# A two-block transformer kernel in split float32: high weights pass once over the operand's high and low halves side by side, and a second, normalised operand

## The chip, the cores and the metric

The kernel runs on one core of one Trainium2 chip, as one launch. The metric is the device time of a launch in microseconds (us), here a median of three. A core has a matrix engine (TensorE, PE in the rows), three engines for elementwise work (VectorE or DVE, ScalarE or ACT, GpSimd or POOL), SyncE (SP), which here only issues the transfers of the weights, a memory SBUF of 128 partitions, and the accumulators of TensorE, PSUM, of which this kernel uses eight banks of 128 x 512 float32.

## The reference

256 tokens, width 1024, feed-forward width 2816, two blocks of two layers each. Every layer is a mixer and a feed-forward, each behind an RMS norm and added to the residual `h`:

```python
def _rmsnorm(x, g):
    return x * lax.rsqrt(jnp.mean(x * x, axis=-1, keepdims=True) + EPS) * g
def _token_mixer(xn, ...):                                   # block 1, both layers
    u, q, k, v, g_pool, g_attn = jnp.split(xn @ w_in, SPLITS, axis=-1)
    pooled = centred means of u over windows (2, 4, 8, 16), a quarter of the width each, minus u
    pool_out = (pooled @ w_pool, group by group) * pool_scale
    attn_out = three dilated local attentions over q, k, v (4 heads of 128 each), mixed by their lse
    return (sigmoid(g_pool) * (pool_out @ w_a) + sigmoid(g_attn) * (attn_out @ w_b)) @ w_o
def _conv_ffn(xn, w_up, conv_w, conv_b, w_down):             # block 2: silu, and a causal convolution
    a, gval = jnp.split(xn @ w_up, 2, axis=-1)
    a = depthwise convolution of a over 3 tokens + conv_b
    return (gelu(a) * gval) @ w_down
```

Block 2 has an even layer (HGRN2 recurrence and an S5 state space side by side) and an odd layer (latent attention) in place of the token mixer.

## The kernel before

Activations lie feature-major: `h` is [128 features, 8 tiles, 256 tokens]. TensorE multiplies in float32r, which keeps fewer bits than float32, so each operand of the large products is a high part and a low part: `X[0]` is the rounded value and `X[1]` what is left, and so with weights. A weight piece of up to 128 x 1024 float32 is fetched by SP's queue (`raw`), ScalarE casts it to the high part `whi` (L170), and VectorE subtracts for the low part `wlo` (L172); each of the three has four buffers. A product is three passes (`mm3`, L187 to L189):

```python
nc.tensor.matmul(out, lhsT=a[0], rhs=b[0], start=start, stop=False)   # high weight, high operand
nc.tensor.matmul(out, lhsT=a[0], rhs=b[1], start=False, stop=False)   # high weight, low operand
nc.tensor.matmul(out, lhsT=a[1], rhs=b[0], start=False, stop=stop)    # low weight, high operand
```

With the weight as the stationary side (128 x 128) and the 256 tokens as moving columns, a weight tile is three matmuls of 256 columns into one half of a bank. `chunkA` does this for two feature tiles of a stage's output (16 weight tiles, 48 matmuls, two pieces of weights). Four banks are there for it. Value projections (`chunkB`) take the tokens as the stationary side and 512 weight columns as moving ones; for the first attention group (`nat`) the tokens stand side by side, for the other two (`par`) they are every second one.

`Norm.feed` makes the operand `X` of the next stage as soon as a tile of `h` is made: h times the norm's gain, split. The factor 1/rms of a token isn't in it. It is known when the last tile is done; `Norm.finish` spreads it over the partitions as `rb` (L296), and whoever takes a result out of PSUM multiplies by `rb` (VectorE), or scales by its column `rs` (the values, ScalarE). So a stage starts without waiting for the norm; its first three chunks (`chunksA`) leave the last two operand tiles to the end. The feed-forward loop over 22 chunks is, for each:

```python
nc.vector.tensor_tensor(ag, ps, bc2(rb), op=ALU.mult)          # L526: both halves, convolution and gate
nc.scalar.activation(c, a, AF.Identity, scale=w[j0], ...)      # L531: middle tap and bias
nc.vector.scalar_tensor_tensor(out=c[:, o], in0=a[:, s_], ...) # L539: twice, the other two taps
nc.scalar.activation(c, c, act)                                # L541
nc.gpsimd.tensor_tensor(c, c, ag[:, 1, :], op=ALU.mult)        # L542: times the gate
nc.scalar.copy(ah[:, i, :], c)                                 # L543: high part
nc.gpsimd.tensor_tensor(al[:, i, :], c, ah[:, i, :], ...)      # L544: low part
```

The down-projection follows: 8 output tiles, 22 weight tiles each, one VectorE addition to `h` (L569), and the feed of the next stage. In the feed-forward of block 1's second layer GpSimd also works through the parameters of S5 (`side`, from L659 on), one or two steps behind each low part. `EdgeNorm` is the norm between the blocks. The tile framework's scheduler sets the order of the instructions on each engine and the semaphores; every engine works through its own list in order.

## Time and profile before

| | |
|---|---|
| timed, median of 3 | 1569.27 us (1568.94 to 1570.26) |
| profiled execution, span from first to last instruction | 1566.8 us |
| what lies between them | 2.5 us |
| TensorE: a matmul under way | 1519.9 us, 97%, 12596 matmuls |
| VectorE busy | 1066.2 us, 68% |
| ScalarE busy | 779.6 us, 50% |
| GpSimd busy | 613.3 us, 39% |
| read from device memory | 256.45 MB, 164 GB/s over the span |

No total is recorded for the profiled execution beside its span, so the median minus the span stands for what lies around it. Busy time is the sum of recorded durations, with overlaps counted once; it is an average over stages that differ, and an engine that is busy half of the span may be the one waited for in a stage of 80 us.

### The profile page before, as it was taken

The page shows a single profiled execution, that of the slowest core. Times are in us where ns is not written, and L with a number is a line of the kernel's source. Part 1 is how long each engine was busy: PE and PEld are TensorE (multiplying, and loading weights), DVE is VectorE, ACT ScalarE, POOL GpSimd, SP SyncE. Part 2 cuts the span into 40 slices and gives each one's busy share as a digit, 9 for nine tenths or more (in the row PEclk, how much of TensorE's full clock was granted, in tenths as well). Part 3 has the DMA queues.
Part 4 walks back from the last instruction along what each step waited for, and adds up shares of the span by engine and source line. Part 5 has one row for each costly group of instructions (what it writes and reads, how often), then busy time and mean ns, then how long its engine had stood idle before and what let it go on. Part 6 is the DMA issues. An engine that isn't in the chain of part 4 may idle for free.

```text
span 1566.8 us, 30996 instructions
## 1 busy us (share of the span) xinstructions
PE 1519.9 (97%) x12596; PEld 1482.1 (95%) x12596; DVE 1066.2 (68%) x1384; ACT 779.6 (50%) x1192; POOL 613.3 (39%) x606
## 2 busy tenths in 40 slices
PE   9999999999999999999988799999999998999997
PEld 8899999999999999999977799999999997999997
DVE  6756566766666566648587587978766667776754
ACT  4644444555444544445544444456555445565542
POOL 5500023333336000224999984444433312333332
PEclk9999999999999999999999999999999999999999
DMA  8554355555464643565443265335554554355553
GB/s 254 188 181 148 127 176 187 186 187 174 159 208 156 219 163 134 169 195 185 150 136 134 88 196 191 109 115 177 188 188 151 184 181 138 106 182 185 172 161 112
DMA packets 90542, 260.07 MB, mean 166 GB/s; under 512 B 17688, under 2 KB 28840, under 8 KB 90400
## 3 DMA queue, kind: packets, MB, share of 16 engines
q1 hardware_dynamic: 78688, 254.05, 49.4%
q10 hardware_dynamic: 11552, 3.73, 1.1%
q8 instruction: 98, 1.61, 0.4%
q14 instruction: 44, 0.36, 0.1%
q0 software_dynamic: 160, 0.32, 0.1%
HBM read 256.45 MB, written 1.10 MB: 164 GB/s over the span
## 4 chain that ended last, share of the span: by engine, by line
PE 77%; POOL 11%; DVE 7%; issue 2%; DMA 1%; ACT 1%; DVEq 0%; ACTq 0%; POOLq 0%
PE ps_mm L187 24%; PE ps_mm L189 24%; PE ps_mm L188 24%; DVE wlo L172 3%; POOL tm L708 1%; POOL al L544 1%; POOL cv L542 1%; DVE xl L247 1%; PE ps_sm L443 1%; POOL s5c L709 1%; POOL s5b L709 1%; ACT whi L170 1%; DVE h L474 1%; POOL s5b L707 1%; POOL s5c L707 1%
## 5 line engine op out<-in xcount | busy, mean ns | idle before, releaser
L172 DVE TENSOR_TENSOR wlo<-raw,whi 128x1024 fp32r<-128x1024 f32 (+3 forms) x536 | 649.8, 1227 | 275.9 <-ACT whi L170 268.4
L170 ACT CAST whi<-raw 128x1024 fp32r<-128x1024 f32 (+3 forms) x536 | 509.7, 958 | 427.0 <-PE ps_mm L188 342.6
L189 PE MATMUL ps_mm<-xh,wlo 128*128 128x256 f32 x2352 | 671.7, 286 | 14.7 <-DVE wlo L172 14.5
L187 PE MATMUL ps_mm<-xh,whi 128*128 128x256 f32 x2352 | 669.6, 285 | 3.4 <-DVE gate L464 1.7
L188 PE MATMUL ps_mm<-xl,whi 128*128 128x256 f32 x2352 | 670.2, 285 | 0.8 <-DVE xl L247 0.8
L189 PEld LDWEIGHTS ps_mm<-xh,wlo 128*128 128x128 f32 x2352 | 453.4, 193 | 18.2 <-DVE wlo L172 18.2
L187 PEld LDWEIGHTS ps_mm<-xh,whi 128*128 128x128 f32 x2352 | 453.6, 193 | 4.8 <-ACT whi L170 3.5
L188 PEld LDWEIGHTS ps_mm<-xl,whi 128*128 128x128 f32 x2352 | 453.7, 193 | 3.2 <-DVE xl L247 2.9
L189 PE MATMUL ps_mm<-ah,wlo 128*128 128x256 f32 x704 | 199.3, 283 | 1.6 <-DVE wlo L172 1.6
L187 PE MATMUL ps_mm<-ah,whi 128*128 128x256 f32 x704 | 199.3, 283 | 0.6 <-ACT whi L170 0.6
L188 PE MATMUL ps_mm<-al,whi 128*128 128x256 f32 x704 | 199.2, 283 | 0.0
L542 POOL TENSOR_TENSOR cv<-cv,ag 128x256 f32<-128x256 f32 x88 | 115.4, 1312 | 211.8 <-ACT cv L541 191.3
L465 POOL TENSOR_TENSOR gate<-gate 128x256 f32<-128x256 f32 x16 | 20.0, 1258 | 343.3 <-DVE gate L464 343.3
L259 POOL TENSOR_TENSOR sq<-h 128x256 f32<-128x256 f32 (+1 forms) x47 | 70.5, 1499 | 184.7 <-DVE h L569 93.4
L189 PEld LDWEIGHTS ps_mm<-ah,wlo 128*128 128x128 f32 x704 | 135.2, 192 | 1.8 <-DVE wlo L172 1.8
L187 PEld LDWEIGHTS ps_mm<-ah,whi 128*128 128x128 f32 x704 | 135.2, 192 | 0.8 <-ACT whi L170 0.8
L188 PEld LDWEIGHTS ps_mm<-al,whi 128*128 128x128 f32 x704 | 135.2, 192 | 0.0
L539 DVE SCALAR_TENSOR_TENSOR cv<-ag,vec,cv 128x255 f32<-128x255 f32 (+1 forms) x176 | 102.0, 579 | 20.1 <-ACT cv L531 17.1
L543 ACT CAST ah<-cv 128x256 fp32r<-128x256 f32 x88 | 35.8, 407 | 136.3 <-POOL cv L542 136.2
L544 POOL TENSOR_TENSOR al<-cv,ah 128x256 fp32r<-128x256 f32 x88 | 75.4, 857 | 34.6 <-ACT ah L543 34.1
L526 DVE TENSOR_TENSOR ag<-ps_mm,rb 128x512 f32<-128x512 f32 x88 | 60.5, 687 | 40.2 <-PE ps_mm L189 39.8
L531 ACT ACTIVATE cv<-ag,vec 128x256 f32<-128x256 f32 x88 | 52.6, 598 | 26.2 <-POOL al L544 18.9
(342 smaller groups left out, 2127.1 us busy)
## 6 DMA issues: line engine op xcount, KB each, us to landing
raw<-w_up SPq DMA_DIRECT2D x88, 512.0 KB, 3.6
raw<-w_fi SPq DMA_DIRECT2D x88, 512.0 KB, 3.7
raw<-w_qk SPq DMA_DIRECT2D x48, 512.0 KB, 3.6
raw<-w_gate SPq DMA_DIRECT2D x32, 512.0 KB, 3.6
raw<-w_down SPq DMA_DIRECT2D x32, 512.0 KB, 3.5
raw<-w_fo SPq DMA_DIRECT2D x32, 512.0 KB, 3.6
raw<-w_v SPq DMA_DIRECT2D x24, 512.0 KB, 4.5
raw<-w_u SPq DMA_DIRECT2D x16, 512.0 KB, 6.0
```

Source lines behind the costliest of these rows:

```text
L170: nc.scalar.copy(self.hi[:, :n], raw[:, :n])
L172: eng.tensor_tensor(self.lo[:, :n], raw[:, :n], self.hi[:, :n].bitcast(F32), op=ALU.subtract)
L187: nc.tensor.matmul(out, lhsT=a[0], rhs=b[0], start=start, stop=False)
L188: nc.tensor.matmul(out, lhsT=a[0], rhs=b[1], start=False, stop=False)
L189: nc.tensor.matmul(out, lhsT=a[1], rhs=b[0], start=False, stop=stop)
L259: nc.gpsimd.tensor_tensor(q, hs, hs, op=ALU.mult)
L526: nc.vector.tensor_tensor(ag, ps, bc2(rb), op=ALU.mult)
L531: nc.scalar.activation(c, a, AF.Identity, scale=w[j0], bias=cb[:, i:i + 1])
L539: nc.vector.scalar_tensor_tensor(out=c[:, o], in0=a[:, s_], scalar=w[j], in1=c[:, o], op0=ALU.mult, op1=ALU.add)
L542: nc.gpsimd.tensor_tensor(c, c, ag[:, 1, :], op=ALU.mult)
L543: nc.scalar.copy(ah[:, i, :], c)
L544: last = nc.gpsimd.tensor_tensor(al[:, i, :], c, ah[:, i, :].bitcast(F32), op=ALU.subtract)
```

## The change

An operand is one tile now, [128, k, 2, 256], with the high and the low part of a feature tile next to each other (`Pair`). Where the weight is the stationary side, `mmW` makes one matmul of 512 columns with the high weight over both parts, and one of 256 with the low weight over the high part: a weight tile is two matmuls. The first lands in both halves of a bank, and the low weight's is put on the right half; `fold` adds the halves at evacuation: ScalarE copies the right half out, VectorE adds it to the left one. A chunk (`chunkW`) fills two banks in place of one. The bank's halves can't be multiplied by `rb` and added in one instruction, so these stages read a second operand, `xn`, that has 1/rms in it already (`normalised`): eight steps on VectorE, ScalarE and GpSimd each, in every stage that has such chunks (two mixers, the even layer, four feed-forwards). The first three chunks of a stage and the pool projections, the merges and the output projections keep the three passes (`mmX`); the values keep their form but read `xn`, and are copied out without a factor. In the down-projection seven of eight output tiles use `mmW`, with two additions to `h` on VectorE (L617 of the change); the eighth keeps the old form. The tags of the large tiles change (`b24` twice becomes `b24` and `c24`).

```diff
+        class Pair:
+            def __init__(self, t):
+                self.t = t
+                self.hl = (t[:, :, 0, :], t[:, :, 1, :])
...
+        def mmW(ps, w, X, k, nk, start=None, stop=None):
+            nc.tensor.matmul(ps, lhsT=w[0], rhs=X.t[:, k].rearrange("p a b -> p (a b)"),
+                             start=k == 0 if start is None else start, stop=False, skip_group_check=True)
+            nc.tensor.matmul(ps[:, S:], lhsT=w[1], rhs=X[0][:, k, :], start=False,
+                             stop=k == nk - 1 if stop is None else stop, skip_group_check=True)
+        def fold(out, ps, view=lambda t: t):
+            t = ap_.tile([128, S], F32, tag="ft", name="ft", bufs=3)
+            nc.scalar.copy(t, ps[:, S:])
+            nc.vector.tensor_tensor(out, view(ps[:, :S]), view(t), op=ALU.add)
...
+        def chunkW(src, X, nk=8):
+            w = Chunk(src, nk * 256)
+            pss = []
+            for m in range(2):
+                pss.append(bank())
+                for k in range(nk):
+                    mmW(pss[m], w.at((m * nk + k) * 128), X, k, nk)
+            return pss
...
+            def normalised(self):
+                Y = split_pair("xn")
+                for k in range(8):
+                    t = ap_.tile([128, S], F32, tag="ft", name="xt", bufs=3)
+                    nc.vector.scalar_tensor_tensor(out=t, in0=h[:, k, :], scalar=self.g[:, k:k + 1], in1=self.rb,
+                                                   op0=ALU.mult, op1=ALU.mult)
+                    nc.scalar.copy(Y[0][:, k, :], t)
+                    nc.gpsimd.tensor_tensor(Y[1][:, k, :], t, Y[0][:, k, :].bitcast(F32), op=ALU.subtract)
+                return Y
...
         def mixer(l, nm):
...
-            rb, rs = nm.rb, nm.rs
+            rb = nm.rb
+            Y = nm.normalised()
...
-            v_group(l, 0, X, rs, qkv)
+            v_group(l, 0, Y, qkv)
...
-                qk_head(l, j, X, rb, qkv)
+                qk_head(l, j, Y, qkv)
...
-            ps = chunkA(A["w_gate"][l, m], X)
             g = ap_.tile([128, 2, S], F32, tag="gate", name="gate", bufs=3)
-            nc.vector.tensor_tensor(g, ps, bc2(rb), op=ALU.mult)
+            for i, ps in enumerate(chunkW(A["w_gate"][l, m], X)):
+                fold(g[:, i], ps)
...
         def ffn(nm, win, cw, cb, wdown, act, shifts, feed, side=None):
...
-            ah = ap_.tile([128, NF, S], F32R, tag="b24", name="ah")
-            al = ap_.tile([128, NF, S], F32R, tag="b24", name="al")
+            Y = nm.normalised()
+            hk = NF // 2
+            act_ = [Pair(ap_.tile([128, hk, 2, S], F32R, tag=t + "24", name="act", bufs=1)) for t in "bc"]
...
-                nc.vector.tensor_tensor(ag, ps, bc2(rb), op=ALU.mult)
+                if i < 3:
+                    nc.vector.tensor_tensor(ag, pss[i], bc2(rb), op=ALU.mult)
+                else:
+                    for j, ps in enumerate(chunkW(win(i), Y)):
+                        fold(ag[:, j], ps)
...
-                    mm3(pd[m][:, :S], w.at(k * 128), (ah[:, kk, :], al[:, kk, :]), kk == 0, kk == NF - 1)
+                    mmd = mmW if m < 7 else lambda ps, *a: mmX(ps[:, :S], *a)
+                    mmd(pd[m], w.at(k * 128), act_[c], k, hk, kk == 0, kk == NF - 1)
...
-                nc.vector.tensor_tensor(h[:, m, :], ps[:, :S], h[:, m, :], op=ALU.add)
+                for o in range(0, 2 * S if m < 7 else S, S):
+                    nc.vector.tensor_tensor(h[:, m, :], ps[:, o:o + S], h[:, m, :], op=ALU.add)
...
             def head_in(hd):
-                ps = chunkA(A["w_eqf"][hd], X) if hd else p0[2]
...
+                if hd:
+                    pss = chunkW(A["w_eqf"][hd], Y)
+                    fold(q[:, hd, :], pss[0])
+                    fold(f, pss[1])
...
-                ps = chunkA(A["w_eg"][c], X)
+                for m, ps in enumerate(chunkW(A["w_eg"][c], Y)):
```

Three places show what the scheduler makes of it. A row is the line, the operation, what it writes and reads, the tile's size, and how many in a row.

VectorE at the start of the first feed-forward layer, behind the sum of squares (`ms`), before:

```order
L285 TENSOR_SCALAR ms<-ps_sm 128x2
L172 TENSOR_TENSOR wlo<-raw,whi 128x1024 x3
L526 TENSOR_TENSOR ag<-ps_mm,rb 128x512
L172 TENSOR_TENSOR wlo<-raw,whi 128x1024
L539 SCALAR_TENSOR_TENSOR cv<-ag,vec,cv 128x255 x2
```

and of the change:

```order
L335 TENSOR_SCALAR ms<-ps_sm 128x2
L172 TENSOR_TENSOR wlo<-raw,whi 128x1024 x3
L313 SCALAR_TENSOR_TENSOR xt<-h,vec,rb 128x256 x3
L569 TENSOR_TENSOR ag<-ps_mm,rb 128x512
L172 TENSOR_TENSOR wlo<-raw,whi 128x1024
L313 SCALAR_TENSOR_TENSOR xt<-h,vec,rb 128x256
L569 TENSOR_TENSOR ag<-ps_mm,rb 128x512
L313 SCALAR_TENSOR_TENSOR xt<-h,vec,rb 128x256
L585 SCALAR_TENSOR_TENSOR cv<-ag,vec,cv 128x255
L313 SCALAR_TENSOR_TENSOR xt<-h,vec,rb 128x256
L172 TENSOR_TENSOR wlo<-raw,whi 128x1024
```

The eight multiplies of the normalised operand (L313) stand between the low parts of the weights and the evacuations of the first three chunks (L569), the last ones behind the first multiply-adds (L585).

ScalarE in the same layer's loop, a chunk and the start of the next, before:

```order
L170 CAST whi<-raw 128x1024
L531 ACTIVATE cv<-ag,vec 128x256
L170 CAST whi<-raw 128x1024
L541 ACTIVATE cv<-cv 128x256
L543 CAST ah<-cv 128x256
L170 CAST whi<-raw 128x1024
```

and of the change:

```order
L577 ACTIVATE cv<-ag,vec 128x256
L170 CAST whi<-raw 128x1024
L219 COPY ft<-ps_mm 128x256
L587 ACTIVATE cv<-cv 128x256
L590 CAST act<-cv 128x256
L170 CAST whi<-raw 128x1024
L219 COPY ft<-ps_mm 128x256
L577 ACTIVATE cv<-ag,vec 128x256
```

Two copies out of PSUM (L219) are in the loop, one of them between the weight cast (L170) and the middle tap (L577). The middle tap needs the addition of VectorE on that copy, which in VectorE's list stands behind the low part of that weight cast; so the loop goes from the cast L590 over L170, VectorE's low part and additions, its two multiply-adds, the activation L587, and GpSimd's multiply to the next L590.

GpSimd at the start of the feed-forward layer of block 1's second layer, before:

```order
L287 TENSOR_TENSOR rs<-ms,nhalf 128x2
L542 TENSOR_TENSOR cv<-cv,ag 128x256
L544 TENSOR_TENSOR al<-cv,ah 128x256
L659 MEMSET s5p 128x16
L660 TENSOR_SCALAR s5p<-s5p 128x16
```

and of the change:

```order
L337 TENSOR_TENSOR rs<-ms,nhalf 128x2
L316 TENSOR_TENSOR xn<-xt,xn 128x256 x7
L588 TENSOR_TENSOR cv<-cv,ag 128x256
L316 TENSOR_TENSOR xn<-xt,xn 128x256
L591 TENSOR_TENSOR act<-cv,act 128x256
L711 MEMSET s5p 128x16
```

Eight subtractions (L316) stand ahead of the first parameter step (the MEMSET of `s5p`), seven of them ahead of the loop's first multiply.

## Rows read from the trace of the kernel before

**Rows 1.** The page: span, and busy us (share) xinstructions of each engine.

```profile
span 1566.8 us, 30996 instructions
PE 1519.9 (97%) x12596; PEld 1482.1 (95%) x12596; DVE 1066.2 (68%) x1384; ACT 779.6 (50%) x1192; POOL 613.3 (39%) x606
```

**Rows 2.** Windows: us, length, busy PE PEld DVE ACT POOL, clock, DMA, GB/s.

```profile
303.80:401.40 97.60, 97.60 (x816) 97.60 (x815) 67.92 (x85) 54.34 (x85) 37.14 (x34) 1.00 0.53 174
```

**Rows 3.** Windows: block 1's second feed-forward layer, and the even layer.

```profile
800.00:884.00 84.00, 67.12 (x610) 63.63 (x609) 57.62 (x51) 37.21 (x61) 84.00 (x78) 0.92 0.36 120
1000.00:1040.00 40.00, 39.12 (x527) 36.56 (x525) 37.19 (x81) 18.45 (x43) 21.17 (x22) 1.00 0.27 93
```

**Rows 4.** Timeline of TensorE, value groups: start us, recorded us, operation, tile.

```profile
490.54 0.39 PE L187 MATMUL ps_mm<-whi,xh 128*128 128x512 f32 x1
...
501.22 0.39 PE L189 MATMUL ps_mm<-whi,xl 128*128 128x512 f32 x1
...
502.87 0.40 PE L187 MATMUL ps_mm<-whi,xh 128*128 128x512 f32 x1
...
513.82 0.40 PE L189 MATMUL ps_mm<-whi,xl 128*128 128x512 f32 x1
```

**Rows 5.** Lines by form, VectorE: count | busy us, mean ns | idle before, releaser.

```profile
L410 DVE TENSOR_TENSOR qkv<-ps_mm,rb 128x256 f32<-128x256 f32 x8 | 3.4, 424 | 3.1 <-PE ps_mm L189 2.8
L606 DVE SCALAR_TENSOR_TENSOR h<-h,vec,rb 128x256 f32<-128x256 f32 x8 | 3.3, 511 | 0.0
```

**Rows 6.** Lines by form, ScalarE and GpSimd.

```profile
L296 ACT COPY rb<-ps_sm 128x256 f32<-128x256 f32 x16 | 5.9, 370 | 3.5 <-PE ps_sm L294 3.5
L544 POOL TENSOR_TENSOR al<-cv,ah 128x256 fp32r<-128x256 f32 x88 | 75.4, 857 | 34.6 <-ACT ah L543 34.1 <-DMA raw<-w_fi 0.5
```

**Rows 7.** Timelines of three engines, a loop of the first feed-forward; [idle before <-releaser].

```profile
309.58 0.41 ACT L543 CAST ah<-cv 128x256 fp32r<-128x256 f32 x1 [1.57 <-POOL cv L542]
309.90 1.04 ACT L170 CAST whi<-raw 128x1024 fp32r<-128x1024 f32 x1
...
310.97 1.22 DVE L172 TENSOR_TENSOR wlo<-raw,whi 128x1024 fp32r<-128x1024 f32 x1 [0.63 <-ACT whi L170]
312.11 0.99 DVE L539 SCALAR_TENSOR_TENSOR cv<-ag,vec,cv 128x255 f32<-128x255 f32 x2
...
313.36 0.41 ACT L541 ACTIVATE cv<-cv 128x256 f32<-128x256 f32 x1
...
313.49 1.23 DVE L172 TENSOR_TENSOR wlo<-raw,whi 128x1024 fp32r<-128x1024 f32 x1 [0.38 <-ACT whi L170]
...
313.85 1.46 POOL L542 TENSOR_TENSOR cv<-cv,ag 128x256 f32<-128x256 f32 x1 [3.04 <-ACT cv L541]
...
315.35 0.41 ACT L543 CAST ah<-cv 128x256 fp32r<-128x256 f32 x1 [1.57 <-POOL cv L542]
```

**Rows 8.** Timelines of VectorE and ScalarE, start of the first feed-forward.

```profile
283.09 3.50 DVE L172 TENSOR_TENSOR wlo<-raw,whi 128x1024 fp32r<-128x1024 f32 x3 [1.67 <-ACT whi L170]
...
284.94 0.37 ACT L296 COPY rb<-ps_sm 128x256 f32<-128x256 f32 x1
...
303.89 0.69 DVE L526 TENSOR_TENSOR ag<-ps_mm,rb 128x512 f32<-128x512 f32 x1 [0.70 <-PE ps_mm L189]
```

**Rows 9.** Timelines of VectorE and GpSimd, block 1's second feed-forward.

```profile
729.01 3.50 DVE L172 TENSOR_TENSOR wlo<-raw,whi 128x1024 fp32r<-128x1024 f32 x3 [1.67 <-ACT whi L170]
...
738.31 0.74 POOL L542 TENSOR_TENSOR cv<-cv,ag 128x256 f32<-128x256 f32 x1 [10.17 <-PE ps_mm L189]
...
740.25 0.11 POOL L659 MEMSET s5p<- 128x16 f32 x1
...
896.35 0.72 POOL L544 TENSOR_TENSOR al<-cv,ah 128x256 fp32r<-128x256 f32 x1
```

**Rows 10.** Timelines of GpSimd and TensorE, the pool groups of the first mixer.

```profile
63.81 1.42 POOL L362 TENSOR_TENSOR pll<-pw,plh 128x512 fp32r<-128x512 f32 x1 [0.52 <-ACT plh L361]
...
66.15 0.28 PE L187 MATMUL ps_mm<-plh,whi 128*128 128x256 f32 x1
```

144 lines of the change are left out of this document (71 added, 73 removed).

## The prediction

> **What bounds the kernel now.** I read the page first. Over the span of 1566.8 us TensorE has a matmul under way for 1519.9 us, 97% [rows 1]. A matmul's recorded duration overlaps the next one's (0.28 us for one of 256 columns [rows 10]), so this says only that there is nearly always one in flight; the rate is read from counts and start times. The window row of the first feed-forward layer's loop has 816 matmuls in 97.6 us, 0.1196 us each, at a granted clock of 1.00 (the 2.4 GHz level), with no idle time [rows 2]. VectorE is busy 67.9 of these 97.6 us, ScalarE 54.3, GpSimd 37.1. So in these stretches what TensorE issues is the time, and what the other engines do is free until it gets in its way. The same view of the other stretches finds two where that is not so. From 800 to 884 us, in the feed-forward layer of block 1's second layer, GpSimd is busy 84.00 of 84.00 us and TensorE has idle time; from 1000 to 1040 us, in the even layer, VectorE is busy 37.19 of 40 us [rows 3].
>
> **What it removes.** A weight tile costs three passes now: 3 x 0.120 = 0.360 us. After the change it costs one pass of 512 columns and one of 256. The trace has 512-column matmuls in the value groups of the mixer: 48 from 490.54 to 501.22, in 47 steps of 0.227 us, where stationary columns lie side by side, and 48 from 502.87 to 513.82, in steps of 0.233, where they are taken two apart [rows 4]. Twice the columns cost 0.227 and not 0.240: about 0.013 us goes with a pass, whatever its width, and one pass per tile disappears. In the new calls the stationary columns are side by side, so I take 0.227 + 0.120 = 0.347 and save 0.013 a tile. If 0.233 held, it would be 0.007; that is the other bound.
>
> Tiles, counted from the code: up-projections 4 layers x 19 chunks x 16 = 1216; down-projections 4 x 7 x 22 = 616; q/k 2 x 4 x 3 x 16 = 384; gates 2 x 8 x 16 = 256; even layer (3 + 2) x 16 = 80. Together 2552, and 2552 x 0.013 = **33.2 us less** (17.9 by the other bound). A feed-forward layer has 458 of them (6.0 us), a mixer 320 (4.2 us).
>
> The Trainium skill, page "TensorE: Matmul & The Clock Gate", section "Back-to-back issue gap", gives N/2.4 + 2.5 ns for a warm pass, 109 and 216 ns here; a tile would go from 328 to 325 ns and the change would save 6.4 us instead of 33.2. The rows, at 120 and 227 ns, contradict it, so the sum goes by the rows.
>
> **What it adds, and what hides it.** (a) Evacuation. For a chunk VectorE had one 512-element multiply; it has two adds of 256 now, nearest row 424 ns each, and ScalarE two copies out of PSUM at 370 ns [rows 5, 6]. Per chunk of 5.55 us (16 x 0.347) VectorE goes from 4.0 (67.9 / 97.6 x 5.77) to 4.2 us and ScalarE from 3.2 to 3.9 us: both still fit, so as load they cost nothing. The second add in a down-projection (28 x 0.42 us) is hidden in the same way; it is on the end chain only for the last tile, which keeps the old form.
>
> But ScalarE's and VectorE's queues are in order, and in the new order (shown above) one loop runs through both and GpSimd. Followed from a cast of one chunk to the next chunk's cast, by rows of the old loop [rows 7]: cast to weight cast 0.32, to the low part 1.07, low part to the next instruction 1.14, add 0.42, two multiply-adds 0.99, activation 0.41, hand-over 0.08, GpSimd's multiply 1.46, hand-over 0.04: 5.93 us. GpSimd's multiply took 1.46 while VectorE made a low part beside it (313.49) and 0.74 without one (738.31) [rows 7, 9]. In the new order about 0.7 us of it meets a low part, so I take 1.3 and 5.77 us; the bounds are 5.2 and 5.93. The chunk takes TensorE 5.55 us, so the loop falls behind by 0.22 us a chunk, 4.0 us over 18. TensorE doesn't feel that at once: there are four banks, so a filled one is wanted again three halves, 8.3 us, later; copy, low part ahead, and add need some 3.1 us of it, and the start (b) eats another 1. That leaves 4. I charge 0.5 us for each of three layers, **+1.5** (0 to 8.5).
>
> (b) The normalised operand, 7 times eight steps: a VectorE multiply (nearest row 511 ns, same shape), a ScalarE cast (0.41) and a GpSimd subtraction (857 ns) [rows 5 to 7]. In a feed-forward layer the row factors arrive at 285.31 (284.94 + 0.37) and the first three chunks, on the old operand, last until 298.1 (the fourth ends at 303.89, less 5.77) [rows 8]. VectorE goes on at 286.6 (283.09 + 3.50) with the eight multiplies, three evacuations, two low parts and three multiply-adds between them: 8 x 0.51 + 3 x 0.69 + 2 x 1.22 + 3 x 0.50 = 10.1 us, to 296.7. Cast (0.41), one GpSimd multiply ahead (up to 1.46) and the last subtraction (0.86) end near 299.5, and TensorE needs that eighth part at 298.1 + 7 x 0.347 = 300.5. So there is no stall, with 1 us to spare; without that cover it would be up to 4 us a layer.
>
> (c) Block 1's second feed-forward layer. GpSimd is the bound from its first multiply, at 738.31, to its last subtraction, at 896.35 [rows 9]; it also works through the S5 parameters there. What TensorE saves in that loop, 304 x 0.013 = 4.0 us, cannot show. And GpSimd starts later: seven of the eight subtractions now stand before its first multiply, which follows VectorE's third multiply-add. From the third low part's end (729.01 + 3.50 = 732.5) VectorE does 7 x 0.51 + 2 x 0.69 + 2 x 1.22 + 3 x 0.50 = 8.9 us, to 741.4; activation 0.41, GpSimd's multiply 0.74, eighth subtraction 0.86, cast 0.41 and first subtraction 0.74 follow, so the parameter work begins near 745, not at 740.25. **+9.0** (0 if the side work is less tight than it looks, 12 if the longer VectorE queue slows GpSimd too).
>
> (d) Even layer. VectorE has 4.1 us more work on an engine that is 93% busy [rows 3], and the value matmuls now wait for the new operand. I charge all of it, **+4.1** (0 to 8).
>
> (e) Mixers. In the first mixer GpSimd makes the four pool groups one after the other, with short pauses such as the 0.52 us in the row, and the last one's low part ends at 65.23 (63.81 + 1.42); TensorE takes it up 12 matmuls after 66.15, at 67.6 [rows 10]. Eight subtractions (8 x 0.86 = 6.9 us) in front, less four such pauses that they fill, bring it to about 70: +2.5. In the other mixer the slack is larger; 0.5. **+3.0** (0 to 6). Value, q/k and gate chunks come later than the operand.
>
> **The sum.** 1566.8 - 33.2 + 1.5 + 9.0 + 4.1 + 3.0 = 1551.2 us of span. The timed median, 1569.27, lies 2.5 us above this execution's span, so **1553.7, said as 1554**. The added costs are 17.6 us, half of what is saved.
>
> **Rivals.** *A: only columns count.* If a 512-column pass cost twice a 256-column one (0.240), a tile would still cost 0.360; nothing is saved, the added work stays: 1569.3 + 17.6 = 1587. Against it: the 0.227 of [rows 4]. The skill's formula named above is nearly this case; its 6.4 us would give 1580. Chance 0.05.
>
> *B: the ScalarE-VectorE-GpSimd loop becomes the bound of the feed-forward layers.* It decides from 5.77 us a chunk; TensorE's gain is gone in all when three layers lose 15.6 us more, 5.2 each, at 5.55 + (4 + 0.5 + 5.2) / 18 = 6.1 us. At 6.4 it would be 3 x (18 x 0.85 - 4) = 34 instead of 1.5: 1586. For it: without the add the same rows sum to 5.51, so the old loop, at 5.77 [rows 7], had 0.26 us to spare, and the add takes more. Against: all its steps are rows, and they sum to 5.93 at most. The Trainium skill, page "SBUF — State Buffer", section "SBUF: two separate sides", says that VectorE and GpSimd lock a shared port pair for a whole instruction, the other blocking fully; the 1.46 beside the 0.74 agrees, and with a full block the loop would be 5.9. Chance of a time above 1566 by it: 0.13.
>
> *C: the added work hides.* If (c), (d) and (e) cost half or less, 1537 to 1546. For it: GpSimd and VectorE have pauses elsewhere. Against: 84.00 of 84.00. Chance 0.13.
>
> *D: a middle of B and the forecast*, the loop at 5.93 with one or two late operands: 1562 to 1572, chance 0.11, of which 0.06 lies within 0.2%.
>
> **How the numbers follow.** The forecast, 1546 to 1562, has 0.58. A change of 0.2% (3.1 us) is about what a measurement of this kernel can tell from none. Below 1566 lie the forecast, C and the rest of D: faster 0.58 + 0.13 + 0.05 = 0.76. Same: 0.06 of D and 0.02 of B, 0.08. Slower: A and what is left of B, 0.16. The range takes D whole, the upper part of C and the lower of B, leaving out some 0.18: 1541 to 1572.
>
> **What would show it.** In the timeline of TensorE a 512-column pass starts 0.227 us and the 256-column pass behind it 0.120 us before the next; a feed-forward chunk takes 5.55 us. 0.24 there is A. In the waits, TensorE waiting for the add into a gate tile, or for a low part, in the three unburdened feed-forward layers for more than some 10 us is B. In the windows, the layer with the S5 parameters should end some 3 us later against its own start than before, the other three 5 us sooner. The prediction is wrong if the operand xn is late at the fourth chunk (TensorE waiting for GpSimd's subtraction), or if the even layer is more than 8 us longer.

## The result, and the profile after

The changed kernel takes 1590.72 us in the median of four runs, against 1569.11 us: a ratio of 1.0136 (95% interval 1.0124 to 1.0148). It is 21.6 us slower where 15 us faster was forecast, and it lies outside the range of 1541 to 1572 us. The profiled execution's span is 1586.7 us, 19.9 more than before.

The page of the changed kernel, which answers to [rows 1]:

```profile
span 1586.7 us, 26515 instructions
PE 1515.4 (96%) x10036; PEld 1356.4 (85%) x10036; DVE 1098.2 (69%) x1576; ACT 856.3 (54%) x1490; POOL 631.3 (40%) x662
```

The change did what it says: 12596 - 10036 = 2560 matmuls fewer, for some 2552 tiles that lost a pass. The busy share doesn't show where the loss is; the stages do. A stage's length is read from the windows between two marks in TensorE's timeline: the transposes that spread a norm's row factors, and the first and last matmul of a down-projection. Windows of the changed kernel, with the columns of [rows 2]: the first mixer, the first feed-forward's up- and down-projection, the second mixer, the even layer, and the last feed-forward's up- and down-projection.

```profile
31.74:298.31 266.57, 256.39 (x1642) 231.69 (x1641) 168.47 (x225) 136.09 (x222) 62.49 (x65) 0.98 0.52 165
298.31:415.58 117.27, 114.95 (x674) 101.88 (x673) 89.44 (x132) 80.79 (x150) 50.02 (x49) 0.99 0.57 180
415.58:476.88 61.30, 61.30 (x377) 55.01 (x376) 36.81 (x55) 28.43 (x43) 12.23 (x17) 1.00 0.61 193
485.35:744.18 258.83, 254.24 (x1671) 231.51 (x1670) 172.04 (x224) 132.89 (x212) 63.46 (x61) 1.00 0.55 171
980.03:1108.80 128.77, 121.83 (x1256) 109.24 (x1255) 110.73 (x202) 63.72 (x124) 55.55 (x56) 0.97 0.36 117
1395.75:1513.24 117.49, 115.20 (x675) 100.82 (x673) 89.37 (x132) 80.23 (x150) 50.34 (x49) 1.00 0.55 180
1513.24:1575.58 62.34, 62.34 (x377) 55.14 (x376) 30.91 (x46) 26.27 (x41) 11.83 (x17) 1.00 0.47 151
```

The same marks in the profiled executions of the kernels below give this table, in us. "Up" and "down" are the sums over the three feed-forwards without the S5 work; "S5 ffn" runs from the norm in front of that feed-forward to the spread behind it, at the start of the even layer.

| kernel | mixer 1 | mixer 2 | up x3 | down x3 | S5 ffn | even | rest | span |
|---|---|---|---|---|---|---|---|---|
| before | 252.8 | 256.2 | 350.8 | 190.1 | 235.4 | 118.7 | 163.0 | 1566.8 |
| changed | 266.6 | 258.8 | 350.2 | 184.9 | 235.9 | 128.8 | 161.5 | 1586.7 |
| down_only | 252.7 | 256.2 | 350.8 | 187.0 | 236.2 | 119.6 | 161.3 | 1563.8 |
| mixers_x | 253.0 | 256.6 | 350.5 | 184.9 | 237.5 | 126.5 | 164.3 | 1573.2 |
| room | 259.9 | 258.9 | 350.2 | 184.9 | 236.0 | 132.6 | 159.0 | 1581.6 |
| room_late | 258.6 | 258.8 | 350.5 | 186.0 | 238.3 | 127.0 | 158.9 | 1578.2 |
| cv3 | 267.2 | 260.9 | 350.4 | 186.0 | 235.9 | 125.3 | 161.3 | 1586.9 |
| mixeven_x | 253.0 | 256.9 | 355.2 | 187.0 | 236.2 | 118.1 | 162.7 | 1569.0 |
| mixeven_five | 253.0 | 256.2 | 345.3 | 187.0 | 237.7 | 117.8 | 162.3 | 1559.4 |
| narrow | 261.6 | 259.3 | 362.8 | 190.1 | 236.5 | 119.9 | 161.0 | 1591.1 |
| even_heads | 253.0 | 256.2 | 345.8 | 187.0 | 237.2 | 127.6 | 162.5 | 1569.3 |
| even_gates | 253.0 | 256.2 | 345.8 | 187.0 | 236.8 | 123.3 | 161.3 | 1563.4 |
| swap | 253.0 | 256.2 | 342.6 | 184.8 | 239.0 | 119.1 | 162.3 | 1557.0 |
| gates_wide | 259.5 | 258.8 | 345.3 | 187.0 | 238.4 | 118.7 | 160.9 | 1568.6 |

Each row is one profiled execution. Executions of one kernel lie up to 8.4 us apart (1583.57 to 1591.98 us in four of `room`), so a difference of a few us between two rows needs the medians beside it. The kernel before has a median of 1568.84 to 1569.11 us in each of the four series of runs, so medians can be compared across them.

Against before, the changed kernel gains 5.2 us in the down-projections and 0.6 in the up-projections, and loses 16.5 in the mixers and 10.1 in the even layer.

**First mixer.** What TensorE waited for from 0 to 300 us, the three longest waits of the changed kernel (total us, times, longest):

```profile
PE ps_mm L187 <- ACT phl L410: 4.1, 1, 4.1
PE ps_mm L189 <- DVE wlo L172: 2.9, 2, 2.5
PE ps_mm L187 <- ACT qkv L443: 2.9, 1, 2.9
```

The first is the projection of the first pool group. The timeline of TensorE in the changed kernel, and that of GpSimd, which makes the low part of that group:

```profile
40.82 0.28 PE L189 MATMUL ps_mm<-x,wlo 128*128 128x256 f32 x1
...
45.16 0.58 PE L187 MATMUL ps_mm<-phl,whi 128*128 128x256 f32 x1 [4.07 <-ACT phl L410]
...
43.93 2.55 POOL L316 TENSOR_TENSOR xn<-xt,xn 128x256 fp32r<-128x256 f32 x2
46.44 1.28 POOL L411 TENSOR_TENSOR phl<-pw,phl 128x512 fp32r<-128x512 f32 x1
```

and the same two in the kernel before:

```profile
41.02 0.28 PE L187 MATMUL ps_mm<-plh,whi 128*128 128x256 f32 x1
...
39.34 1.86 POOL L362 TENSOR_TENSOR pll<-pw,plh 128x512 fp32r<-128x512 f32 x1 [0.93 <-ACT plh L361]
```

That low part started at 39.34 before and at 46.44 now: the eight multiplies (VectorE) and subtractions (GpSimd, L316) of the new operand are spread among the pool groups' steps, two of the subtractions right in front of it. TensorE had no time in hand there at all. The third wait is a bank of the values that ScalarE doesn't copy out, because it stands in order behind casts of the bias tables that wait for a transfer. ScalarE in the changed kernel:

```profile
75.95 1.00 ACTq L376 DMA_DIRECT2D room<-scr  x2
79.37 0.51 ACT L381 CAST th<-room 128x384 fp32r<-128x384 f32 x1 [2.92 <-DMA room<-scr]
```

In the kernel before, ScalarE cast the first piece of these tables at 28.41 us, beneath the start of the mixer. Their work space `room` is one of two large operand buffers now, and both are taken until X is free. After these waits the granted clock was lower for a stretch; windows of the changed kernel (before, both had 1.00):

```profile
40.00:60.00 20.00, 15.93 (x71) 13.25 (x70) 13.88 (x15) 8.05 (x13) 16.39 (x22) 0.83 0.44 139
80.00:100.00 20.00, 19.58 (x87) 16.52 (x88) 12.84 (x16) 14.31 (x24) 0.00 (x0) 0.91 0.68 220
```

**Start of a feed-forward.** In the first feed-forward of the changed kernel, TensorE's first wide pass and GpSimd's last subtraction for the operand:

```profile
305.95 0.40 PE L212 MATMUL ps_mm<-xn,whi 128*128 128x512 f32 x1
...
312.67 0.92 POOL L316 TENSOR_TENSOR xn<-xt,xn 128x256 fp32r<-128x256 f32 x1
```

A bank of a wide chunk sums over all eight parts of the operand, so none is complete before 313.59, 7.6 us after the first wide pass; in order, TensorE would have come to the eighth tile after 7 x 0.347 = 2.4 us. It doesn't stand still for that: in its list the tiles of the four banks follow each other as the parts arrive. But so the first full bank comes late. ScalarE and TensorE of the changed kernel where the fourth chunk's first bank is full and waits to be emptied:

```profile
316.62 0.42 ACT L587 ACTIVATE cv<-cv 128x256 f32<-128x256 f32 x1 [1.19 <-DVE cv L585]
316.95 1.03 ACT L170 CAST whi<-raw 128x1024 fp32r<-128x1024 f32 x1
317.88 0.36 ACT L219 COPY ft<-ps_mm 128x256 f32<-128x256 f32 x1
...
317.03 0.27 PE L214 MATMUL ps_mm<-xn,wlo 128*128 128x256 f32 x1
319.62 0.71 PE L212 MATMUL ps_mm<-xn,whi 128*128 128x512 f32 x1 [2.32 <-DVE ag L220]
```

and a window right behind that wait, for the granted clock:

```profile
319.62:322.00 2.38, 2.38 (x7) 2.04 (x8) 2.38 (x3) 2.38 (x5) 1.67 (x1) 0.53 0.71 186
```

The first copy out of a wide bank (L219) stands in ScalarE's list behind the activations and casts of the first three chunks. Those are late because VectorE and GpSimd had the operand's steps in between. TensorE has filled all four banks by 317.03, waits 2.3 us, and runs near the lower of its two levels, 1.2 GHz, for the next 3 us (0.53 in this window). The clock does not fall behind every such wait. In the last feed-forward, TensorE's wait and a window right behind it:

```profile
1417.04 0.50 PE L212 MATMUL ps_mm<-xn,whi 128*128 128x512 f32 x1 [2.29 <-DVE ag L220]
1417.30:1419.70 2.40, 2.40 (x15) 2.08 (x15) 2.40 (x3) 2.40 (x4) 1.42 (x1) 1.00 0.76 234
```

That layer's up-projection is no shorter all the same (117.49 us against 117.27): its passes run at 0.176 us a matmul (498 in 87.49 us) against 0.173, two rates that the last section comes back to. Behind the wait of the first layer there is no other; the loop, which answers to [rows 2] and [rows 7], in a window of the changed kernel:

```profile
330.00:410.00 80.00, 80.00 (x463) 70.56 (x463) 58.78 (x89) 56.59 (x105) 32.99 (x32) 1.00 0.58 184
```

TensorE is busy for all of it, 463 matmuls in 80 us, 0.1728 us each, 5.53 us for the 32 of a chunk.

### The profile page after: what moved, and what is told of

Same layout as the page of the kernel before. It is cut to its first block, busy times and chain, and to the rows that moved or that the text cites. A ratio compares the mean times of both kernels' runs of the same rounds, so it can differ in the third digit from the quotient of the medians.

```text
span 1586.7 us, 26515 instructions
## 1 busy us (share of the span) xinstructions
PE 1515.4 (96%) x10036; PEld 1356.4 (85%) x10036; DVE 1098.2 (69%) x1576; ACT 856.3 (54%) x1490; POOL 631.3 (40%) x662
## 5 line engine op out<-in xcount | busy, mean ns | idle before, releaser
L212 PE MATMUL ps_mm<-xn,whi 128*128 128x512 f32 x1936 | 694.5, 402 | 21.1 <-DVE ag L220 20.5
L170 ACT CAST whi<-raw 128x1024 fp32r<-128x1024 f32 (+3 forms) x536 | 507.8, 958 | 361.5 <-PE ps_mm L212 203.2
L214 PE MATMUL ps_mm<-xn,wlo 128*128 128x256 f32 x1936 | 548.1, 284 | 0.0
L212 PEld LDWEIGHTS ps_mm<-xn,whi 128*128 128x128 f32 x1936 | 368.6, 191 | 108.4 <-DVE ag L220 24.0
L214 PEld LDWEIGHTS ps_mm<-xn,wlo 128*128 128x128 f32 x1936 | 371.6, 192 | 1.1
L212 PE MATMUL ps_mm<-act,whi 128*128 128x512 f32 x616 | 215.2, 394 | 0.0
L214 PE MATMUL ps_mm<-act,wlo 128*128 128x256 f32 x616 | 173.1, 281 | 1.4 <-DVE wlo L172 1.4
L585 DVE SCALAR_TENSOR_TENSOR cv<-ag,vec,cv 128x255 f32<-128x255 f32 (+1 forms) x176 | 106.4, 607 | 36.5 <-ACT cv L577 33.9
L188 PE MATMUL ps_mm<-x,whi 128*128 128x256 f32 x416 | 120.8, 291 | 1.9 <-DVE x L288 1.8
L189 PE MATMUL ps_mm<-x,wlo 128*128 128x256 f32 x416 | 119.4, 288 | 2.9 <-DVE wlo L172 2.9
L187 PE MATMUL ps_mm<-x,whi 128*128 128x256 f32 x416 | 119.2, 288 | 0.0
L214 PEld LDWEIGHTS ps_mm<-act,wlo 128*128 128x128 f32 x616 | 116.5, 189 | 2.4 <-DVE wlo L172 2.4
L219 ACT COPY ft<-ps_mm 128x256 f32<-128x256 f32 x242 | 87.7, 362 | 0.0
L188 PEld LDWEIGHTS ps_mm<-x,whi 128*128 128x128 f32 x416 | 81.1, 195 | 3.9 <-DVE x L288 3.9
L187 PEld LDWEIGHTS ps_mm<-x,whi 128*128 128x128 f32 x416 | 81.1, 195 | 0.0
```

Of the source, the lines that this page charges most:

```text
L170: nc.scalar.copy(self.hi[:, :n], raw[:, :n])
L212: nc.tensor.matmul(ps, lhsT=w[0], rhs=X.t[:, k].rearrange("p a b -> p (a b)"), start=k == 0 if start is None else start, stop=False, skip_ ...
L214: nc.tensor.matmul(ps[:, S:], lhsT=w[1], rhs=X[0][:, k, :], start=False, stop=k == nk - 1 if stop is None else stop, skip_group_check=True)
L219: nc.scalar.copy(t, ps[:, S:])
L585: nc.vector.scalar_tensor_tensor(out=c[:, o], in0=a[:, s_], scalar=w[j], in1=c[:, o], op0=ALU.mult, op1=ALU.add)
```

## The experiments

Each verdict is the ratio to the kernel before on the same chip. Stages are named as in the table.

**1. The down-projections alone.** The kernel before, with

```diff
-                    mm3(pd[m][:, :S], w.at(k * 128), (ah[:, kk, :], al[:, kk, :]), kk == 0, kk == NF - 1)
+                    if m < 7:
+                        mmW(pd[m], w.at(k * 128), act_[c], k, kk == 0, kk == NF - 1)
```

with the activation's high and low parts side by side in one tile, and the two additions behind it.

> The kernel before with the two-pass form in the down-projections alone (seven of eight output tiles, no normalised operand, no copy on ScalarE). Theory: a pass costs some 13 ns beside its columns, so each of the 616 tiles goes from 0.360 us to 0.347, 8.2 us less, near 1561 us; a down-projection takes 61.3 us instead of 63.4. Rival, only the columns count: 0 us, 1569. Rival, the second addition on VectorE delays the next stage's operand: 1567 or more, with the gain in the down-projection and the loss behind it.

Measured: 1565.51 us, ratio 0.9981 (0.9973 to 0.999), so 3 us and not 8. A down-projection takes 62.33 us in all three places, not 61.3. Two rates are possible, then: with the eighth tile at 22 x 0.360 = 7.92 us, a wide tile costs (62.33 - 7.92) / 154 = 0.353 us here and (61.30 - 7.92) / 154 = 0.347 in the first feed-forward of the changed kernel. Both are below 63.36 / 176 = 0.360: "only the columns count" is refuted, and the gain is half of what was forecast where the slower rate holds. The second addition delays nothing: mixer 2, which begins behind one, has its old length.

**2. The mixers as before.** The changed kernel with block 1's mixers on X, three passes, and `rb` at evacuation.

```diff
-            v_group(l, 0, Y, qkv)
+            v_group(l, 0, X, rs, qkv)
...
-                qk_head(l, j, Y, qkv)
+                qk_head(l, j, X, rb, qkv)
```

> The changed kernel with block 1's two mixers as before (operand X, three passes, factor at evacuation); the even layer and the feed-forwards keep the change. Theory: the mixers lost 16.5 us by waits for the operand, the bias tables and their buffers and for the clock behind each, so the time falls from 1590.7 to about 1574. Rival, the loss lies in the two-step evacuations wherever they are: the mixers have 640 of 2552 tiles, so some 5 us return, 1586.

Measured: 1573.33 us, ratio 1.0022 (1.0012 to 1.0032). The mixers take 253.0 and 256.6 us again; 17 of the 21.6 us are theirs, with a quarter of the tiles.

**3. The bias tables' work space in memory of its own.**

```diff
-            room = ap_.tile([128, 4, 1024], F32, tag="hl", name="room", bufs=2)
+            room = sp.tile([128, 2, 1024], F32, name="room", bufs=1)
```

> The changed kernel with the work space of the bias tables in memory of its own instead of one of the two large operand buffers. Theory: in the first mixer the tables wait for the operand X to come free, their transfers and casts then stand in ScalarE's list in front of the copies of the values, and TensorE waits 3 us for a bank with its clock low behind it; with memory of its own the tables are made under the start as before: 5 to 8 us less, near 1584. Rival, the first mixer's loss is the late second operand alone: no more than 1.5 us, 1589.

Measured: 1587.55 us, ratio 1.0119 (1.0102 to 1.0135), 3.2 less in the median. The first mixer gets 6.7 us shorter (266.6 to 259.9), as the theory had it; the even layer of this profile is 3.8 us longer, at which the edit does nothing, so its length varies between kernels by that much, and this profiled execution (1583.57) lies 4.0 us under the median of the four. The wait for a bank of the values is gone. So is the one of 4.1 us for the first pool group, but TensorE now stands nearly as long at the same place for a bias table:

```profile
43.73 0.69 PE L384 MATMUL ps_aux<-th,flipr 128*128 128x384 f32 x1 [3.70 <-DVE th L382]
```

From 80 to 100 us the clock is whole again:

```profile
80.00:100.00 20.00, 20.00 (x107) 17.20 (x106) 10.12 (x14) 11.13 (x18) 0.00 (x0) 1.00 0.60 195
```

**4. The operand behind the pool groups as well, in the program.**

```diff
             P[3] = pool_group(l, 3, ps3, rb)
+            Y = nm.normalised()
```

> The changed kernel with the bias tables in memory of their own, and with the normalised operand of a mixer made behind the four pool groups instead of ahead of them. Theory: the rest of the first mixer's loss, 7 us, is the pool projections that wait for low parts behind the operand's subtractions in GpSimd's list (4.1 us) and the clock that falls behind that; with the operand later this part goes, 4 to 7 us less than 1587.5, near 1582. Rival, the values then wait for the operand instead: 1587 or more.

Measured: 1580.41 us, ratio 1.0086 (1.0065 to 1.0108). The mixer itself gains only 1.3 us (258.6). The scheduler did not leave the operand behind the pool groups: in VectorE's list three of its eight multiplies stand ahead of the last step there of the first group (34.52), the other five ahead of that of the second (45.59).

```profile
30.97 2.47 DVE L313 SCALAR_TENSOR_TENSOR xt<-h,vec,rb 128x256 f32<-128x256 f32 x3
```

The first group's low part starts at 36.48 now, and at 43.22 in 3. The wait of 3.70 us for a bias table is gone, and others have come in; TensorE's waits of this kernel from 28 to 287 us begin with:

```profile
PE ps_mm L188 <- DVE wlo L172: 2.9, 4, 1.1
```

These are matmuls of the values, which wait for low parts of their weights. The first of them (0.70 us, at 43.32) has two multiplies of the operand right ahead of that low part in VectorE's list; the later ones have a late cast or a bias table's step there. So the rival is half right: the values wait, but not for the operand. The theory's kernel, with the operand made behind the groups, was not run. The other 6 us of the median lie outside the mixer and are not explained by the edit.

**5. A third buffer for the convolution's result.**

```diff
-                c = ap_.tile([128, S], F32, tag="cv", name="cv", bufs=2)
+                c = ap_.tile([128, S], F32, tag="cv", name="cv", bufs=3)
```

> The changed kernel with three buffers instead of two for the convolution's result cv. Theory: at a feed-forward's start the middle tap of the third chunk waits for a cv buffer, which GpSimd frees late because it still makes the normalised operand; the copy that empties the bank of the fourth chunk stands behind it in ScalarE's list, and TensorE waits 2.3 us and runs at half clock for as long again. With a third buffer this goes in three layers, 3 x 4 = 12 us less, near 1579. Rival, the queues of VectorE and ScalarE are simply too long at that point: less than 1 us a layer, 1588 or more.

Measured: 1586.24 us, ratio 1.0112 (1.0099 to 1.0125). The up-projections together are unchanged (350.4), and the wait at each start is 1.8 us instead of 2.3. The theory fell: the buffer is not the cause. The median is 4.5 us below the changed kernel's, but the two profiled executions are equal (1586.9 and 1586.7), so no stage shows where that comes from. The edit holds for every tile with this tag, in other stages too.

**6. Mixers and even layer as before.** As 2, and the even layer's chunks on X (`chunkA`, with `rb`).

> The changed kernel with block 1's mixers and block 2's even layer as before; only the feed-forwards keep the change. Theory: the norm between the blocks and the even layer together were 12 us longer with the change, since VectorE, ScalarE and GpSimd get the eight steps of the operand in front of a chain that they set; without it 1573.3 falls to about 1561. Rival, the even layer starts late because the feed-forward in front of it, with the S5 parameters on GpSimd, hands its work over late: then it stays long, and no more than 4 us return, 1569.

Measured: 1567.91 us, ratio 0.9993 (0.9981 to 1.0005): no difference from before. That is 5.4 us less than in 2, between the theory's 12 and the rival's 4. The even layer has its old length (118.1). The up-projections are 4.5 us longer than before, with wide passes: the wait at the start is there, and in this execution (1570.94, 3.0 us above the median of ten) all three run at the slower of the two rates; they are 5.0 us longer than the changed kernel's.

**7. Five chunks on the old operand.** As 6, and

```diff
-                if i < 3:
-                    nc.vector.tensor_tensor(ag, pss[i], bc2(rb), op=ALU.mult)
+                if i < 5:
+                    nc.vector.tensor_tensor(ag, pss[i] if i < 3 else chunkA(win(i), X), bc2(rb), op=ALU.mult)
```

> As the kernel with mixers and even layer as before, and the first five chunks of a feed-forward instead of three on the old operand with three passes. Theory: the first copy out of a wide bank stands in ScalarE's list behind the casts of the first three chunks, which wait for GpSimd, which still makes the normalised operand; two chunks later that has cleared. TensorE's wait of 2.3 us and its half clock behind it go in three layers, 3 x 3.7 = 11 us less than with three chunks, about 1550. Rival, the wait only moves two chunks back: no difference, 1561. The third buffer for cv shortened the wait from 2.3 to 1.8 us only, so that buffer was not the cause.

Measured: 1561.48 us, ratio 0.9958 (0.9943 to 0.9973). The up-projections are 9.9 us shorter than in 6 (345.3 against 355.2), near the 11 expected; TensorE waits for nothing in the first of them. By layer it is 3.7 and 3.9 us, where the clock fell behind the wait in 6, and 2.3 in the last, where it stayed at 1.00. The wait did not move back: two chunks later the operand is complete and the backlog of the start has cleared. Which of the two counts, the run doesn't separate. The median fell by 6.4 us, less than the profiled span's 9.6.

**8. Three passes over the new operand.** The changed kernel with `chunkW` in one bank and three passes, and one copy on VectorE as evacuation; down-projections as before.

```diff
-            nc.scalar.copy(t, ps[:, S:])
-            nc.vector.tensor_tensor(out, view(ps[:, :S]), view(t), op=ALU.add)
+            nc.vector.tensor_copy(out, view(ps))
```

> The changed kernel with three passes of 256 columns wherever it had the two, over the same normalised operand, and one copy on VectorE in place of ScalarE's copy and VectorE's addition; down-projections with one addition. Theory: the wide pass itself pays, 7 to 13 ns a tile, and the loss is the operand's and the buffers': then this kernel is 15 to 30 us slower than the changed one, near 1610. Rival, the two-step evacuation and the doubled banks cost what the passes save: 1585 to 1595.

Measured: 1593.21 us, ratio 1.0156 (1.0139 to 1.0173). The rival's number came out: undoing the wide pass everywhere costs 2.5 us and not 20. But the stages take the sum apart. The wide passes are worth 12.6 us in the up-projections (362.8 to 350.2) and 5.2 in the down-projections, and cost 5.0 in mixer 1 and 8.9 in the even layer. The second operand without any wide pass, with the buffers that it takes, costs 12.0 us in the mixers, 12.0 in the up-projections and 1.2 in the even layer. So the operand's price was the larger mistake. In the first feed-forward TensorE's longest wait here is for the operand itself:

```profile
PE ps_mm L188 <- POOL xn L313: 1.0, 1, 1.0
```

Of the even layer's loss little is the operand's; four kernels with that layer wholly changed have 126.5 to 132.6 us for it, all above the 119.9 here.

**9 and 10. Heads or gates of the even layer.** On the kernel of 7, with the even layer changed, but for its heads' chunks in one and its gates' in the other, which have three passes on `xn`:

```diff
-                    pss = chunkW(A["w_eqf"][hd], Y)
-                    fold(q[:, hd, :], pss[0])
-                    fold(f, pss[1])
+                    ps = chunkA(A["w_eqf"][hd], Y)
+                    nc.vector.tensor_copy(q[:, hd, :], ps[:, 0, :])
+                    nc.vector.tensor_copy(f, ps[:, 1, :])
```

```diff
-                for m, ps in enumerate(chunkW(A["w_eg"][c], Y)):
+                ps = chunkA(A["w_eg"][c], Y)
+                for m in range(2):
```

> Mixers as before, five chunks on the old operand in the feed-forwards, the even layer on the normalised operand with its heads' chunks in three passes and its gates in two. From the end of the feed-forward before it to the even layer's last norm it took 134.0 us before, 147.4 with the even layer wholly changed, 137.3 with the second operand and three passes throughout. Theory: VectorE sets this stage, and the heads' two-step evacuation lengthens its chain: with the heads back, 138 to 140 us here and some 1565 us in all. Rival, the gates that come earlier in VectorE's list hold the heads up: 145 or more here, 1570.

> The same with the gates' chunks of the even layer in three passes and the heads' in two. Theory (the heads' evacuations): 145 us or more from the end of the feed-forward to the last norm, some 1570 us in all. Rival (the gates ahead in VectorE's list): 138 to 140 us there, 1565.

Measured: 1571.37 us, ratio 1.0015 (1.0006 to 1.0024), with the heads narrow, and 1568.02, ratio 0.9994 (0.9985 to 1.0003), with the gates narrow. From the end of the feed-forward to the last norm it is 146.7 and 141.6 us. The theory fell: with the heads narrow nothing is won. Four kernels with the even layer wholly changed have 146.2 to 152.2 us between these marks, so 146.7 is no gain. The gates' 141.6 is one, but not the rival's 138 to 140, and its execution (1565.31) lies 2.7 us under the median of ten. Between the medians of the two runs, ten executions each, lie 3.4 us: the gates in two passes cost more than the heads. A window of the changed kernel, from the first head's norm to the second's:

```profile
1016.00:1048.00 32.00, 31.30 (x329) 27.18 (x327) 31.45 (x61) 17.98 (x40) 15.40 (x15) 1.00 0.34 107
```

and the same stretch in the kernel of 8:

```profile
1017.60:1046.60 29.00, 28.31 (x362) 26.63 (x360) 28.08 (x58) 12.97 (x28) 14.37 (x15) 1.00 0.31 107
```

VectorE (the third busy figure) sets this stretch: 31.45 of 32.00 us, and 28.08 of 29.00 with three passes. VectorE's timeline of the changed kernel has three additions (L220) and two products (L997) of the gates inside this stretch, of which this is the first; in the kernel of 8 there are none.

```profile
1040.91 0.42 DVE L220 TENSOR_TENSOR eg<-ps_mm,ft 128x256 f32<-128x256 f32 x1
```

So the gates come ahead of a part of the heads' chain in VectorE's list. But that this place is what they cost is not shown, and 9 and 10 speak against it. With the gates narrow two of their copies and two products still stand in this stretch, here the copies, while with the heads narrow there are only one addition and one product:

```profile
1027.16 0.75 DVE L1002 COPY eg<-ps_mm 128x256 f32<-128x256 f32 x2
```

**11. The order of the two passes.** The kernel of 7, where every second tile, but for the last of a bank, has its narrow pass first.

```diff
+            if swap:
+                nc.tensor.matmul(ps[:, S:], lhsT=w[1], rhs=X[0][:, k, :], start=False, stop=False, skip_group_check=True)
             nc.tensor.matmul(ps, lhsT=w[0], rhs=X.t[:, k].rearrange("p a b -> p (a b)"), start=first, stop=False,
                              skip_group_check=True)
+            if not swap:
```

> The kernel with only the feed-forwards changed and five chunks on the old operand, and in every second weight tile the pass of 256 columns ahead of the pass of 512. The traces show two steady rates for the two passes, 0.3465 us a tile and 0.353 (a pattern that repeats after three tiles), and a stretch keeps the one that it fell into. If a pass costs its columns and a fixed 10 to 13 ns, the order changes nothing: 61.3 or 62.3 us for a down-projection, 1561. If the rate hangs on which pass follows which, the down-projections leave these two values, up to 1 us each.

Measured: 1558.81 us, ratio 0.9936 (0.9922 to 0.9949), the fastest of all here. A down-projection takes 61.59 us, a third value, (61.59 - 7.92) / 154 = 0.3485 us a tile, the same in all three layers. So the rate does hang on which pass follows which.

```profile
398.55:460.14 61.59, 61.59 (x376) 54.83 (x375) 37.75 (x55) 29.28 (x44) 13.17 (x17) 1.00 0.61 195
```

**12. Only the mixers' gates on the new operand.** The kernel of 7 with

```diff
+            Y = nm.normalised()
             qk_head(l, 0, X, rb, qkv)
...
-            g = {0: gates(l, 0, X, rb), 1: gates(l, 1, X, rb)}
+            g = {0: gates(l, 0, Y), 1: gates(l, 1, Y)}
```

> The best kernel so far (only the feed-forwards changed, five chunks on the old operand, 1561.5 us) with the gates of block 1's mixers, which come last there, in two passes on a normalised operand that is made behind the values, and the bias tables in memory of their own. Theory: where the operand has 80 us to be made and VectorE has room, the two passes pay: 256 tiles x 7 to 13 ns, 1.7 to 3.4 us less, near 1559. Rival, the gates' shorter chunks no longer cover the last attention head, whose softmax TensorE then waits for, as in the changed kernel (3.8 us of gaps there instead of 1.1): 1562 or more.

Measured: 1570.5 us, ratio 1.001 (1.0001 to 1.0018), 9 us worse than without. The first mixer is 6.5 us longer (259.5 against 253.0), and the second 2.6, which is the changed kernel's whole loss there, though only the gates are changed. The operand is not made behind the values, where the program has it. In the second mixer, which starts at 477.88, VectorE has its first three multiplies at

```profile
480.16 1.27 DVE L313 SCALAR_TENSOR_TENSOR xt<-h,vec,rb 128x256 f32<-128x256 f32 x3
```

and the last at 491.46, among the steps of the first pool groups; so the theory, an operand that has 80 us to be made, was not tested. TensorE's longest waits from 471 to 732 us:

```profile
PE ps_mm L188 <- DVE wlo L172: 1.4, 2, 0.9
PE ps_sm L493 <- DVE p L490: 0.8, 1, 0.8
```

The first line is two waits for low parts of the values' weights. In VectorE's list one of these stands behind the operand's last multiply (TensorE goes on at 493.67), the other behind a step of a pool group (509.98). The next line is the last attention head's softmax, as the rival said; the scheduler has the gates' chunks ahead of it and little is left to cover it.

## Why the prediction was wrong, step by step

In spans the forecast was -15.6 us and the result +19.9, 35.5 apart: 21.8 in the mixers, 10.6 in the three plain feed-forwards, 7.0 in the even layer, and -2.5 and -1.5 in the S5 feed-forward and the rest.

**A tile costs 0.347.** The mechanism was right, rival A was not: the pass that disappears had a price beside its columns. Its size, 13 ns, holds in some stretches; others run at 0.353, 7 ns, which is the other bound that the prediction took from [rows 4]. The three down-projections saved 5.2 us of a forecast 6.0. The Trainium skill, page "TensorE: Matmul & The Clock Gate", section "Back-to-back issue gap", gives N/2.4 + 2.5 ns as the gap of an isolated warm pass; for these widths that makes 216 and 109 ns, an estimate of 325 ns a tile. The runs show 0.347 to 0.353 us a tile, and 0.120 a narrow pass before; the measurement decides.

**(a) The loop through three engines.** It kept up with TensorE (5.53 us a chunk with no wait), so rival B is refuted.

**(b) "There is no stall, with 1 us to spare."** This step failed, by a row of [rows 8] that was taken for the wrong chunk. VectorE's evacuations in the first feed-forward before start at 286.71, 289.68, 293.34, 298.82 and 303.89, so 303.89 is the fifth and not the fourth. The third and the fourth:

```profile
293.34 0.68 DVE L526 TENSOR_TENSOR ag<-ps_mm,rb 128x512 f32<-128x512 f32 x1
...
298.82 0.68 DVE L526 TENSOR_TENSOR ag<-ps_mm,rb 128x512 f32<-128x512 f32 x1
```

The sum had TensorE at the fourth chunk 13.6 us behind the spread of the row factors (298.1 - 284.53). In the changed kernel it is there after 7.6 (305.95 - 298.31), and would need the eighth part at 10.1. The other half of the sum was right: the operand was forecast to be complete after 15.0 us (299.5 - 284.53) and was after 15.3 (313.59 - 298.31). So it was 5 us late by the prediction's own reckoning. The sign that it gave, TensorE waiting for the subtraction, came in one of the four feed-forwards only (0.7 us, block 2's first): TensorE went on in other banks, filled all four, and then waited 2.3 us for a copy that stands in ScalarE's list behind the work that the operand's steps had pushed back. Without that start, experiment 7 is 9.9 us shorter in three layers (6.4 by the medians). The steps were dearer too; in the changed kernel, lines by form:

```profile
L313 DVE SCALAR_TENSOR_TENSOR xt<-h,vec,rb 128x256 f32<-128x256 f32 x48 | 31.6, 684 | 1.0 <-ACT rb L346 1.0
L316 POOL TENSOR_TENSOR xn<-xt,xn 128x256 fp32r<-128x256 f32 x56 | 56.2, 1019 | 50.3 <-ACT xn L315 50.3
```

684 and 1019 ns against the 511 and 857 of [rows 5] and [rows 6]. The 684 is a mean of two kinds: about two thirds of these multiplies took 0.47 to 0.50 us, and about one third, each with a GpSimd instruction beside it, 0.94 to 1.27.

**(c) S5 feed-forward.** GpSimd was busy for 83.78 of the 84 us from 800 to 884, as in [rows 3]:

```profile
800.00:884.00 84.00, 71.14 (x379) 59.72 (x377) 67.47 (x67) 43.03 (x78) 83.78 (x69) 0.91 0.42 134
```

The stretch to the spread behind it took 235.9 us instead of 235.4, where -6.0 + 9.0 = +3.0 was forecast. That TensorE's saving can't show there was right. The later start came too:

```profile
760.26 0.11 POOL L711 MEMSET s5p<- 128x16 f32 x1
...
908.16 0.73 POOL L591 TENSOR_TENSOR act<-cv,act 128x256 fp32r<-128x256 f32 x1
```

The first parameter step is 16.1 us behind the spread in front (744.18), 6.3 later than before, where 4.8 was forecast. What failed is that the rest would keep its length. From there to the last low part it took 147.9 us, against 156.1 before [rows 9], with 162 instructions of GpSimd instead of 175: part of the parameter work now runs behind the loop.

**(d) Even layer.** Forecast -1.0 + 4.1, measured +10.1, more than the 8 us that the prediction named as a sign of being wrong. The term charged the operand's work on VectorE and put the two-step evacuations at nothing. By experiment 8 it is the other way round: the operand without wide passes costs 1.2 us here, the wide passes with their evacuations 8.9. By 9 and 10 the gates have the larger part in that; how, and why heads and gates don't add up, stays open.

**(e) Mixers.** Forecast -8.3 + 3.0, measured +16.5. This is the step that decided. It looked at the last pool group [rows 10], which had 2 us in hand; the first one had none, and TensorE stood 4.1 us in front of it. It left out that the bias tables had lost their buffers, which the whole diff shows (`tag="hl"`, two buffers for X, `xn` and `room`): 6.7 us of that stage by the profiles of experiment 3, 3.2 us in all by the medians. It took the values', q/k and gate chunks as safe because they come later than the operand; but making it holds up low parts of the weights in VectorE's list, and the last attention head lost its cover (experiments 4 and 12). Of mixer 1 another 5.9 us beyond before remain with both edits of experiment 4; they are not split further.

Common to (b) and (e): each looked at one place, the eighth part of the operand and the last pool group, and asked whether that came in time. Neither asked what the new steps push back in the same engines' lists.

## What to carry to other kernels

A pass saved on a bound TensorE is worth its fixed part, here 7 to 13 ns, only where nothing in front of it can stall; a single wait of 2.3 us cost 2.3 us where the clock stayed and 3.9 where it fell, as much as some 175 to 300 tiles save at the higher of these. So put such a change where no new operand is needed (the down-projections here), let the first chunks of a stage run on what is there already until the engines have caught up, and leave alone stages that another engine sets. When buffers change their size or number, look for everything that shared them, the set-up work too. Where a step stands in the program doesn't say where it stands in an engine's list: in experiments 4 and 12 the scheduler made the operand early all the same. And count the rows from the first before one is taken for the fourth: (b) hung on that.

## What the hardware showed that was not expected

The same pair of passes (512, then 256 columns, each with its own weights) ran at one of two steady rates at the same granted clock of 1.00, and a stretch kept the one that it fell into. The timeline of TensorE in the changed kernel, a down-projection of the first feed-forward and, behind "...", one of the last:

```profile
430.14 0.39 PE L212 MATMUL ps_mm<-act,whi 128*128 128x512 f32 x1
430.37 0.28 PE L214 MATMUL ps_mm<-act,wlo 128*128 128x256 f32 x1
430.49 0.39 PE L212 MATMUL ps_mm<-act,whi 128*128 128x512 f32 x1
...
1530.20 0.40 PE L212 MATMUL ps_mm<-act,whi 128*128 128x512 f32 x1
1530.44 0.28 PE L214 MATMUL ps_mm<-act,wlo 128*128 128x256 f32 x1
1530.56 0.40 PE L212 MATMUL ps_mm<-act,whi 128*128 128x512 f32 x1
```

0.347 us a tile in the one, 0.353 on average in the other, where start times repeat after three tiles, (1531.26 - 1530.20) / 3. With every second pair turned round it was 0.3485 in all three down-projections. What makes a stretch fall into one or the other was not found.
